# S5 and modulation transfers moved to the queues of the engines that produce the data, and one overlapping transfer per page of response matrices, in a kernel of two transformer blocks

## The chip, the cores and the metric

One NeuronCore of one Trainium2 chip. The metric is the device time of one execution in microseconds (us); several runs give a median.

## The reference, cut to what matters

The input is a sequence of 512 tokens of width 1024, in float32. The first block modulates its two normalisations by a projection of the condition c, and between them runs a hybrid of three mixers: S5 (a diagonal state space model of 32 groups, 16 channels and 64 states each), MLA (low-rank attention with 8 heads) and a spatial gating unit. Their outputs are gated and projected. The second block has dilated attention, mLSTM and feed-forward parts, and is not touched.

```python
mod = silu(c) @ w_ada + b_ada              # six rows of 1024
proj = h @ w_in + b_in
u_s5, cq, ckv, k_pe, u_sgu, v_sgu, gate_logits = split(proj)
h_t = a * h_(t-1) + bb @ u_t               # S5, complex, per group
y_s5 = real(c @ h_t) + d * u
z = gelu(y_s5);  out = z * sigmoid(z @ w_glu + b_glu)
merged = sum over the branches of gates[b] * (y[b] @ w_branch[b])
return merged @ w_out
```

## The kernel before, in words

**Products in three passes.** Each float32 operand is split in a high part `whi` (ACT, L300) and a rest `wlo` (mostly DVE, L306), and each product is three matmuls (L315 to L317). Weights come as 512 KB pages `raw` (SP, L334). The large projections are written `fm` (features on the partitions) and `tm` (tokens on the partitions).

**How the order comes about.** The program is written out in Python, and each engine works through its own list in that order. The large projections are the foreground. Beside them run background generators (`Bg`, L44): at each piece of foreground matmul work the next step of each is written, up to its next `yield`; a rate of 1.0 makes two plain yields for 12 fm matmuls, and `yield 3` asks for a longer distance. S5, the modulation rows and the attention are three such generators. So what a generator writes stands, on each engine, between the casts and evictions of the foreground and of the other generators. Where an instruction has to wait, all that stands behind it on the same engine waits too. A pool of 36 pages of 4 KB per partition, 8 PSUM banks and 8 small tiles (`t2`) is used in turn: a new page waits for the last reader of the old one.

**Modulation.** `ada_rows` (L1118 to L1159) makes three rows of 1024 (parts j = 4, 3, 2). A part has eight steps k: a 128 x 1024 page `adaw` of w_ada is loaded (512 KB, SP, L1130), ACT multiplies it by a column of the condition (L1145), POOL adds it to `adaacc` (L1146), and the load of the next page is written behind that add. Two matmuls with ones (L1151) then sum over the partitions, DVE adds 1 or 0 (L1157), and SP stores the row (L1158). `ada_join` (L1161) combines two rows with the norm's gains and stores them (L1174). The first two parts run during the S5 stretch, the third in the attention. `ada_gen` (L1074 ff) makes other rows of the same matrix at about 656 to 715 us; its loads are issued by POOL (L1088).

**S5.** `s5_params` (L1196 ff) computes powers of the eigenvalues and the response of a step, `s5k`, which SP stores into the DRAM tile `s5kd` (L1366). The foreground's u5 projection is stored as `s5ud` by ACT. `s5_main` (L1425) reads it back in two halves h, 8 loads of 64 KB each (`s5u`, SP, L1523). For each half `g_pe` multiplies it into the states (`s5g`, L1440), DVE turns and scans, and `y_pe` forms the output `psy`: 16 matmuls with the response matrices `s5m` (L1490), and 32 with the states (L1497); the trace lists each of these matmuls, and those of s5g, twice. The response matrix of a page is a block triangle: `responses` (L1475) has POOL clear the page (L1478) and SP load eight pieces of growing height from `s5kd` (L1481), 16 loads per half. `y_el` copies `psy` on ACT (`s5ys`, L1508) and SP stores it in eight pieces (`s5yd`, L1510); `y_in` (L1517) reads the result back as `s5yf`.

**Gates and attention.** The foreground of this stretch are the 24 gate rows: fm matmuls, a tanh on ACT (`gt`, L2030) and a store that ACT issues (`gates`, L2031). `mla_gen` (L1706) loads its weights (`wvr` by POOL, L1715; `wmr` by SP), splits the value weights (`wvs`, ACT L1749 and DVE L1751), forms the values (`mv`), and then, per head, queries `mq` and keys `mk`, the rotation on DVE and POOL (`rsh`, `mqf`, L1659, L1660), the scores `ms`, and the softmax `mp` on ACT (L1829).

**Completion of transfers.** The transfers that SP and ACT issue share eight completion counters, taken in the order of the program: an issue waits for the one eight before it, whichever of the two engines issued that. By their place in that round the eighth and the ninth s5u load wait for the two gates stores that the program has just ahead of them, on ACT.

Of the kernel before, what the change touches and what calls it, by code (L numbers as in the profile page):

```python
# [16 lines left out]
P = 128  # L17
# [938 lines left out]
class Block1(Core):  # L956
# [161 lines left out]
    def ada_rows(self, parts, fused):  # L1118


        nc = self.nc
        wv = self.ins["w_ada"][0].rearrange("(k p) n -> p k n", p=P)
        loads = []

        def load(n):
            if n < len(parts) * KD:
                i, k = divmod(n, KD)
                j = parts[i][0]
                w = self.page(name="adaw")
                nc.sync.dma_start(w[:, :D], wv[:, k, j * D : (j + 1) * D])  # L1130
                loads.append(w)

        load(0)
        for i, (j, plus, row) in enumerate(parts):
            acc = self.page(name="adaacc")
            nc.gpsimd.memset(acc[:, :D], 0.0)
            nc.gpsimd.dma_start(acc[0:1, :D], self.ins["b_ada"][0:1, j * D : (j + 1) * D])
            for k in range(KD):
                yield
                w = loads.pop(0)  # L1140
                c = self.ccol[:, k : k + 1]
                if fused:
                    nc.vector.scalar_tensor_tensor(acc[:, :D], w[:, :D], c, acc[:, :D], op0=ALU.mult, op1=ALU.add)
                else:
                    nc.scalar.activation(w[:, :D], w[:, :D], AF.Copy, scale=c)  # L1145
                    nc.gpsimd.tensor_tensor(acc[:, :D], acc[:, :D], w[:, :D], op=ALU.add)  # L1146
                load(i * KD + k + 1)
                yield 4 if k == KD - 1 else 0
            pss = [self.ps("adac") for _ in range(2)]
            for half in range(2):  # L1150
                nc.tensor.matmul(  # L1151
                    pss[half][0:1, :], self.ones[:, 0:1], acc[:, half * 512 : half * 512 + 512], start=True, stop=True
                )
            yield
            for half in range(2):
                r = self.t2(name="adar")[0:1, :]
                nc.vector.tensor_scalar(r, pss[half][0:1, :], plus, None, op0=ALU.add)  # L1157
                nc.sync.dma_start(row[:, half * 512 : half * 512 + 512], r)  # L1158
            yield  # L1159

    def ada_join(self, sc, sh):  # L1161

        nc = self.nc
        z = self.t2(name="adaz")[:8].rearrange("b (i p) -> b i p", i=4)
        for i, src in enumerate((sc, sh, self.ins["ln1_g"], self.ins["ln1_b"])):
            nc.sync.dma_start(z[:, i, :], src[0].rearrange("(b p) -> b p", p=P))
        yield
        yield 4
        yield
        nc.vector.tensor_tensor(z[:, 3, :], z[:, 0, :], z[:, 3, :], op=ALU.mult)  # L1170
        nc.vector.tensor_tensor(z[:, 1, :], z[:, 1, :], z[:, 3, :], op=ALU.add)
        nc.vector.tensor_tensor(z[:, 0, :], z[:, 0, :], z[:, 2, :], op=ALU.mult)
        for i, dst in enumerate((sc, sh)):
            nc.sync.dma_start(dst[0].rearrange("(b p) -> b p", p=P), z[:, i, :])  # L1174
        yield

    def vec_cols(self):
# [18 lines left out]
    def s5_params(self):  # L1196
# [137 lines left out]
            nc.vector.tensor_tensor(pw[:, 1, :, m + 1 : 2 * m + 1], x0[:, 1], x1[:, 0], op=ALU.add)  # L1334
        yield
        self.s5W = [[], []]
        self.s5kd = self.dr.tile([P, 512], F32, name="s5kd")
        for h in range(2):
            w, parts = self.s5_powers(h, 0, t0, t1, False)
            for f in parts:  # L1340
                yield
                f()
                yield 3
            for c in range(2):

                pss = [self.ps("s5wt") for _ in range(2)]
                for i in range(8):
                    nc.tensor.transpose(
                        pss[i // 4][:, i % 4 * P : i % 4 * P + P], w[c][:, i].rearrange("p k c -> p (k c)"), self.ident
                    )  # L1350
                if c == 0:
                    pk = [self.ps("s5k") for _ in range(2)]
                    for i in range(8):
                        for g in range(2):
                            hs = slice(64 * g, 64 * g + 64)
                            for e in range(2):
                                nc.tensor.matmul(
                                    pk[g][:, i : P : 8], w[e][hs, i].rearrange("p k c -> p (k c)"),
                                    cc[hs, e, 8 * h + i, :], start=e == 0, stop=e == 1,
                                )  # L1360
                yield
                if c == 0:
                    kk = self.t2(256, name="s5k")
                    for g in range(2):
                        nc.scalar.copy(kk[:, P * g : P * g + P], pk[g][:, :P])
                    nc.sync.dma_start(self.s5kd[:, 256 * h : 256 * h + 256], kk)  # L1366
                pg = self.page([P, 8, P], name="s5W")
                for j in range(2):
                    nc.scalar.copy(pg[:, 4 * j : 4 * j + 4].rearrange("p i s -> p (i s)"), pss[j])
                self.s5W[c].append(pg)  # L1370
                yield
            del w
# [52 lines left out]
    def s5_main(self, uf, ud, yd, yf):  # L1425
# [1 line left out]


        nc = self.nc
        U, V, M, G, A, B, Y = [], None, {}, {}, {}, {}, {}  # L1430
        tabs, cc, W = self.s5_tab, self.s5cc, self.s5W
        del self.s5_tab, self.s5cc, self.s5W

# [37 lines left out]
            nc.vector.tensor_tensor(A[h][:, 1], A[h][:, 1], B[h][:, 0], op=ALU.add)  # L1471
            del B[h]

        def responses(h):

            for g in range(2):
                M[g] = self.page([P, P, 8], name="s5m")
                nc.gpsimd.memset(M[g], 0.0)  # L1478
                ks = slice(256 * h + P * g, 256 * h + P * g + P)
                for t in range(8):  # L1480
                    nc.sync.dma_start(  # L1481
                        M[g][16 * (7 - t) :, 16 * t : 16 * t + 16, :],
                        self.s5kd[: 16 * t + 16, ks].rearrange("p (c i) -> p c i", i=8),
                    )

        def y_pe(h):
            Y[h] = [self.ps("psy") for _ in range(2)]
            for i in range(8):
                for g in range(2):
                    nc.tensor.matmul(  # L1490
                        Y[h][g][:, 64 * i : 64 * i + 64], M[g][:, :, i], U[h][:, 2 * i + g, :], start=i == 0, stop=False
                    )
            for i in range(8):
                for c in range(2):
# [8 lines left out]
        def y_el(h):  # L1503
# [3 lines left out]
            for g, y in enumerate(Y.pop(h)):  # L1507
                nc.scalar.copy(yv[:, g], y.rearrange("p (i n) -> p i n", i=8))  # L1508
            for t in range(8):
                nc.sync.dma_start(  # L1510
                    yd[256 * h : 256 * h + 256, 64 * t : 64 * t + 64].rearrange("(g c) n -> c g n", c=16),
                    ys[16 * t : 16 * t + 16],
                )
# [6 lines left out]
        for h in range(2):  # L1520
            U.append(self.page([P, 16, 64], name="s5u"))
            for s in range(8):
                nc.sync.dma_start(  # L1523
                    U[h][16 * (7 - s) : 16 * (8 - s)],
                    ud[256 * h : 256 * h + 256, 64 * s : 64 * s + 64].rearrange("(g c) n -> c g n", c=16),
                )
        yield 3
        for h in range(2):
            g_pe(h)
# [8 lines left out]
        for h in range(2):  # L1538
# [5 lines left out]
            yield 3  # L1544
            yield
            vs[1]()
            responses(h)
            yield 3
            y_pe(h)
            yield  # L1550
            y_el(h)
            del V, vs, A[h]
            if h == 0:
# [152 lines left out]
    def mla_gen(self, prep, res):  # L1706
# [30 lines left out]
                wsp[p] = (hi, lo)  # L1737

        load_w(0)
        yield  # L1740

        kps = [self.page([P, 2, 512], name="kT") for _ in range(2)]
# [1420 lines left out]
```

## Time and profile before

| | us |
|---|---|
| median of 3 runs | 2568.47 |
| lowest and highest | 2568.18, 2572.43 |
| the profiled execution | 2567.72 |
| its span in the trace | 2566.0 |

Share of the span in which each engine was busy: PE 95%, weight loads of PE 78%, DVE 50%, ACT 37%, POOL 12%. The mean granted clock of TensorE is 0.97 of full speed. The profiled execution lies 0.75 us under the median; 1.7 us of it lie outside the span. An engine's share is an average over 2566 us; the change touches the stretch from about 60 to 420 us, so the timelines and windows of that stretch are the views to read, and times in them are counted from the span's start.

### The profile page before, as it was taken

The numbers are of one execution on the slowest core, as the hardware profiler recorded it, in microseconds if no ns is written. First come the engines' busy times: TensorE is split into PE (matmuls) and PEld (weight loads), VectorE is DVE, ScalarE is ACT, GpSimd is POOL, SyncE is SP. The second block draws the span as 40 slices with busy tenths as digits, with TensorE's granted clock in tenths as the row PEclk, the third lists the DMA queues.
The fourth block names the chain that finished last, engine by engine and source line by source line (L and its number), as shares of the span: only waits on it lengthen the run. The fifth ranks groups of instructions, "written<-read, shape, count | busy, mean of one in ns | idle before, by whom it ended". The sixth has DMA issues, their size and how long they took to land.

```text
span 2566.0 us, 31035 instructions
## 1 busy us (share of the span) xinstructions
PE 2433.2 (95%) x11944; PEld 2008.4 (78%) x11944; DVE 1284.2 (50%) x2169; ACT 958.9 (37%) x1648; POOL 299.9 (12%) x340
## 2 busy tenths in 40 slices
PE   6967689998899999999999999999999999999998
PEld 5866567677788888888888888888888767888887
DVE  6775434468544438555545555333345556432333
ACT  4342245633222234555445453222233444322231
POOL 1032242001200000112111110000000232000000
PEclk9987789999899999999999999999999999999999
DMA  9243443363333325232323343233232214323321
GB/s 299 73 146 112 126 147 106 99 203 117 117 110 105 91 87 168 60 100 81 100 78 93 91 116 99 78 117 90 81 120 66 58 50 131 107 80 110 96 73 53
DMA packets 336149, 271.62 MB, mean 106 GB/s; under 512 B 33234, under 2 KB 288870, under 8 KB 336000
## 3 DMA queue, kind: packets, MB, share of 16 engines
q1 hardware_dynamic: 328832, 252.78, 32.8%
q0 software_dynamic: 3168, 9.51, 1.1%
q10 hardware_dynamic: 4000, 7.34, 0.8%
q8 instruction: 94, 1.54, 0.3%
q14 instruction: 55, 0.45, 0.1%
HBM read 252.50 MB, written 12.87 MB: 103 GB/s over the span
## 4 chain that ended last, share of the span: by engine, by line
PE 83%; DVE 8%; ACT 3%; issue 2%; DMA 2%; POOL 2%; SPq 1%; ACTq 0%; DVEq 0%; POOLq 0%
PE fm L315 16%; PE fm L316 16%; PE fm L317 16%; PE tm L315 9%; PE tm L317 9%; PE tm L316 8%; DVE wlo L306 1%; PE mo L1867 1%; PE ms L1805 1%; PE psy L1490 1%; PE ao L2534 1%; PE as L2408 1%; PE tr L750 1%; PE psy L1497 1%; DMA adaw<-in_w_ada_dram 1%
## 5 line engine op out<-in xcount | busy, mean ns | idle before, releaser
L315 PE MATMUL fm<-xT,whi 128*128 128x512 f32 (+1 forms) x1744 | 664.9, 381 | 0.3 <-ACT xT L300 0.2
L317 PE MATMUL fm<-xT,wlo 128*128 128x512 f32 (+1 forms) x1744 | 658.8, 378 | 4.4 <-DVE wlo L306 4.4
L316 PE MATMUL fm<-xT,whi 128*128 128x512 f32 (+1 forms) x1744 | 657.7, 377 | 0.8 <-DVE xT L306 0.7
L306 DVE TENSOR_TENSOR wlo<-raw,whi 128x1024 fp32r<-128x1024 f32 (+4 forms) x445 | 485.2, 1125 | 81.0 <-ACT whi L300 48.8
L300 ACT CAST whi<-raw 128x1024 fp32r<-128x1024 f32 (+3 forms) x447 | 393.5, 920 | 140.4 <-PE tm L316 50.4
L317 PEld LDWEIGHTS fm<-xT,wlo 128*128 128x128 f32 x1744 | 331.9, 190 | 67.2 <-DVE wlo L306 4.6
L315 PEld LDWEIGHTS fm<-xT,whi 128*128 128x128 f32 x1744 | 332.4, 191 | 62.6 <-issue 1.5
L316 PEld LDWEIGHTS fm<-xT,whi 128*128 128x128 f32 x1744 | 332.2, 191 | 60.9 <-DVE xT L306 1.5
L902 DVE TENSOR_TENSOR sl<-sl,fm 128x512 f32<-128x512 f32 x66 | 45.4, 688 | 426.6 <-PE fm L317 414.0
L315 PE MATMUL tm<-whi,hid 128*128 128x512 f32 x528 | 208.5, 395 | 0.0
L317 PE MATMUL tm<-whi,hid 128*128 128x512 f32 x528 | 207.8, 394 | 0.0
L316 PE MATMUL tm<-wlo,hid 128*128 128x512 f32 x528 | 207.6, 393 | 0.0
L901 ACT ACTIVATE sl<-fm 128x512 f32<-128x512 f32 x66 | 39.5, 599 | 383.7 <-PE fm L317 383.7
L317 PEld LDWEIGHTS tm<-whi,hid 128*128 128x128 f32 x528 | 99.2, 188 | 23.3
L316 PEld LDWEIGHTS tm<-wlo,hid 128*128 128x128 f32 x528 | 99.2, 188 | 22.9
L315 PEld LDWEIGHTS tm<-whi,hid 128*128 128x128 f32 x528 | 99.1, 188 | 22.9
L315 PE MATMUL tm<-whi,xT 128*128 128x384 f32 (+1 forms) x320 | 113.8, 356 | 0.0
L317 PE MATMUL tm<-whi,xT 128*128 128x384 f32 (+1 forms) x320 | 111.5, 348 | 0.0
L316 PE MATMUL tm<-wlo,xT 128*128 128x384 f32 (+1 forms) x320 | 111.3, 348 | 0.0
L315 PE MATMUL fm<-hT,whi 128*128 128x512 f32 x256 | 110.1, 430 | 0.7 <-ACT whi L300 0.7
L317 PE MATMUL fm<-hT,wlo 128*128 128x512 f32 x256 | 103.9, 406 | 7.2 <-DVE wlo L306 7.2
L300 ACT CAST hid<-sl 128x512 fp32r<-128x512 f32 x66 | 41.0, 621 | 186.8 <-DVE sl L902 186.8
(588 smaller groups left out, 3448.3 us busy)
## 6 DMA issues: line engine op xcount, KB each, us to landing
raw<-in_ffn_w_in_dram SPq DMA_DIRECT2D x264, 256.0 KB, 3.4
raw<-in_ffn_w_out_dram SPq DMA_DIRECT2D x69, 512.0 KB, 3.6
raw<-in_attn_w_in_dram SPq DMA_DIRECT2D x96, 256.0 KB, 3.4
adaw<-in_w_ada_dram SPq DMA_DIRECT2D x40, 512.0 KB, 5.9
raw<-in_w_in_dram SPq DMA_DIRECT2D x36, 512.0 KB, 4.8
raw<-in_attn_w_in_dram SPq DMA_DIRECT2D x96, 128.0 KB, 2.7
raw<-in_mlstm_w_in_dram SPq DMA_DIRECT2D x24, 512.0 KB, 3.8
gates<-gt ACTq DMA_DIRECT2D x24, 256.0 KB, 3.7
```

The costliest lines, as they stand in the source:

```text
L300: nc.scalar.copy(hi, src)
L306: f = lambda: eng.tensor_tensor(lo, src, hi.bitcast(F32), op=ALU.subtract)
L315: nc.tensor.matmul(out, a[0], b[0], start=start, stop=False)
L316: nc.tensor.matmul(out, a[0], b[1], start=False, stop=False)
L317: nc.tensor.matmul(out, a[1], b[0], start=False, stop=stop)
L750: self.nc.tensor.transpose(ps[:, (k - k0) * P : (k - k0 + 1) * P], src[:, k * P : (k + 1) * P], self.ident)
L901: nc.scalar.activation(s, ps[0], AF.Silu)
L902: nc.vector.tensor_tensor(s, s, ps[1], op=ALU.mult)
L1490: nc.tensor.matmul(Y[h][g][:, 64 * i : 64 * i + 64], M[g][:, :, i], U[h][:, 2 * i + g, :], start=i == 0, stop=False)
L1497: nc.tensor.matmul(Y[h][g][:, 64 * i + 1 : 64 * i + 64], V[c][hs, i].rearrange("p k c -> p (k c)"), A[h][hs, c, 64 * i : 64 * i + 63], sta ...
L1805: nc.tensor.matmul(ss_[i][:, :n], qts[h][:96, t * P : t * P + P], kts(h)[:, :n], start=True, stop=True)
L1867: nc.tensor.matmul(ops_[h][:, b * P :], vst[b][:, ds], pts_.pop(j), start=b == 0, stop=b == NT - 1)
```

## The change

Five things are done; lines are those of the changed kernel.

1. The 24 loads `adaw` are issued by POOL (L1130), each behind the add of the page before. The row is drained by ACT (L1158, L1160) instead of DVE and stored by ACT (L1161); the two stores of `ada_join` are issued by POOL (L1177).
2. The two stores of `s5k` are issued by ACT (L1373).
3. `s5kd` gets 112 rows of zeros ahead of its 128 (POOL clears and stores them once). `load_m` loads one page `s5r` with one transfer of 512 KB whose rows overlap in DRAM: partition p of block t begins at row p + 16 t. SP issues two of them for the first half right behind the s5u loads, and two for the second half behind the first `y_pe` (L1487). `responses` copies a page to `s5m` with the order of the columns changed (ACT, L1492) instead of POOL's clearing and 16 loads per half; the stationary operand of the matmul is contiguous.
4. The 16 stores `s5yd` are issued by ACT (L1520), behind its copies.
5. `mla_gen` has two more yields, one of them long, behind its first weight load.

```diff
                 w = self.page(name="adaw")
-                nc.sync.dma_start(w[:, :D], wv[:, k, j * D : (j + 1) * D])
+                nc.gpsimd.dma_start(w[:, :D], wv[:, k, j * D : (j + 1) * D])
...
                 r = self.t2(name="adar")[0:1, :]
-                nc.vector.tensor_scalar(r, pss[half][0:1, :], plus, None, op0=ALU.add)
-                nc.sync.dma_start(row[:, half * 512 : half * 512 + 512], r)
+                if plus:
+                    nc.scalar.activation(r, pss[half][0:1, :], AF.Identity, bias=self.ones[0:1, 0:1])
+                else:
+                    nc.scalar.copy(r, pss[half][0:1, :])
+                nc.scalar.dma_start(row[:, half * 512 : half * 512 + 512], r)
...
-            nc.sync.dma_start(dst[0].rearrange("(b p) -> b p", p=P), z[:, i, :])
+            nc.gpsimd.dma_start(dst[0].rearrange("(b p) -> b p", p=P), z[:, i, :])
...
-        self.s5kd = self.dr.tile([P, 512], F32, name="s5kd")
+
+        self.s5kd = self.dr.tile([112 + P, 512], F32, name="s5kd")
+        z = self.t2(name="s5z")[:112]
+        nc.gpsimd.memset(z, 0.0)
+        nc.gpsimd.dma_start(self.s5kd[:112], z)
...
-                    nc.sync.dma_start(self.s5kd[:, 256 * h : 256 * h + 256], kk)
+                    nc.scalar.dma_start(self.s5kd[112:, 256 * h : 256 * h + 256], kk)
...
-        def responses(h):
+        def load_m(h):
 
             for g in range(2):
-                M[g] = self.page([P, P, 8], name="s5m")
-                nc.gpsimd.memset(M[g], 0.0)
-                ks = slice(256 * h + P * g, 256 * h + P * g + P)
-                for t in range(8):
-                    nc.sync.dma_start(
-                        M[g][16 * (7 - t) :, 16 * t : 16 * t + 16, :],
-                        self.s5kd[: 16 * t + 16, ks].rearrange("p (c i) -> p c i", i=8),
-                    )
+                R[g] = self.page([P, 8, P], name="s5r")
+                src = self.s5kd[:P, 256 * h + P * g : 256 * h + P * g + P]
+                (r, _), (c, _) = src.ap
+                nc.sync.dma_start(R[g], bass.AP(src.tensor, src.offset, [[r, P], [16 * r, 8], [c, P]]))
+
+        def responses():
+            for g in range(2):
+                M[g] = self.page([P, 8, P], name="s5m")
+                nc.scalar.copy(
+                    M[g].rearrange("p i (t c) -> p t c i", t=8), R[g].rearrange("p t (c i) -> p t c i", i=8)
+                )
...
-                        Y[h][g][:, 64 * i : 64 * i + 64], M[g][:, :, i], U[h][:, 2 * i + g, :], start=i == 0, stop=False
+                        Y[h][g][:, 64 * i : 64 * i + 64], M[g][:, i, :], U[h][:, 2 * i + g, :], start=i == 0, stop=False
...
-                nc.sync.dma_start(
+                nc.scalar.dma_start(
                     yd[256 * h : 256 * h + 256, 64 * t : 64 * t + 64].rearrange("(g c) n -> c g n", c=16),
...
+        load_m(0)
         yield 3
...
-            responses(h)
+            responses()
...
+            if h == 0:
+                load_m(1)
             y_el(h)
...
         load_w(0)
+        yield
+        yield 3
         yield
```

Three places in the engines' lists. First POOL, where `ada_rows` begins; before:

```order
L1136 MEMSET adaacc_1201 128x1024
L1137 DMA adaacc_1201<-in_b_ada_dram 1x16x64
L1146 TENSOR_TENSOR adaacc_1201<-adaacc_1201,adaw_1199 128x1024
L1146 TENSOR_TENSOR adaacc_1201<-adaacc_1201,adaw_1218 128x1024
L1146 TENSOR_TENSOR adaacc_1201<-adaacc_1201,adaw_1260 128x1024
L1146 TENSOR_TENSOR adaacc_1201<-adaacc_1201,adaw_1302 128x1024
```

and with the change:

```order
L1130 DMA adaw_1202<-in_w_ada_dram 128x1024
L1136 MEMSET adaacc_1204 128x1024
L1137 DMA adaacc_1204<-in_b_ada_dram 1x16x64
L1146 TENSOR_TENSOR adaacc_1204<-adaacc_1204,adaw_1202 128x1024
L1130 DMA adaw_1221<-in_w_ada_dram 128x1024
L1146 TENSOR_TENSOR adaacc_1204<-adaacc_1204,adaw_1221 128x1024
L1130 DMA adaw_1263<-in_w_ada_dram 128x1024
L1146 TENSOR_TENSOR adaacc_1204<-adaacc_1204,adaw_1263 128x1024
L1130 DMA adaw_1305<-in_w_ada_dram 128x1024
```

Each add is now followed by the load of the page that the next add needs.

Second ACT, from the last gates store ahead of the second part of `ada_rows` up to the copies for the first half's `psy`. Before:

```order
L2031 DMA gates<-gt_1728 128x512
L1145 ACTIVATE adaw_1502<-adaw_1502,ccol 128x1024
L300 CAST cqT_1737<-cT_1708 128x512
L1145 ACTIVATE adaw_1735<-adaw_1735,ccol 128x1024
L300 CAST cqT_1766<-cT_1745 128x512
L300 CAST whi_1769<-raw_1511 128x1024
L1145 ACTIVATE adaw_1764<-adaw_1764,ccol 128x1024
L300 CAST cqT_1799<-cT_1778 128x512
L1145 ACTIVATE adaw_1797<-adaw_1797,ccol 128x1024
```

and with the change:

```order
L2046 DMA gates<-gt_1735 128x512
L1145 ACTIVATE adaw_1505<-adaw_1505,ccol 128x1024
L300 CAST cqT_1744<-cT_1715 128x512
L1145 ACTIVATE adaw_1742<-adaw_1742,ccol 128x1024
L300 CAST cqT_1773<-cT_1752 128x512
L300 CAST whi_1776<-raw_1514 128x1024
L1145 ACTIVATE adaw_1771<-adaw_1771,ccol 128x1024
L300 CAST cqT_1806<-cT_1785 128x512
L1492 COPY s5m_1814<-s5r_1534 128x128x8
L1492 COPY s5m_1816<-s5r_1536 128x128x8
L1145 ACTIVATE adaw_1804<-adaw_1804,ccol 128x1024
```

The two copies from `s5r` to `s5m` stand behind three scales of `adaw`.

Third SP, from the s5u loads to the response matrices of the first half. Before:

```order
L1523 DMA s5u_1513<-s5ud 16x16x64 x8
L1523 DMA s5u_1522<-s5ud 16x16x64 x8
L334 DMA raw_1609<-in_w_in_dram 128x4x256
L1158 DMA adarow_265<-adar_1687 1x512
L1158 DMA adarow_265<-adar_1690 1x512
L334 DMA raw_1698<-in_w_in_dram 128x4x256
L1130 DMA adaw_1735<-in_w_ada_dram 128x1024
L1130 DMA adaw_1764<-in_w_ada_dram 128x1024
L334 DMA raw_1772<-in_w_in_dram 128x4x256
L1130 DMA adaw_1797<-in_w_ada_dram 128x1024
L1481 DMA s5m_1807<-s5kd 16x128
L1481 DMA s5m_1807<-s5kd 32x128
```

and with the change:

```order
L1533 DMA s5u_1516<-s5ud 16x16x64 x8
L1533 DMA s5u_1525<-s5ud 16x16x64 x8
L1487 DMA s5r_1534<-s5kd 128x8x128
L1487 DMA s5r_1536<-s5kd 128x8x128
L334 DMA raw_1616<-in_w_in_dram 128x4x256
L334 DMA raw_1705<-in_w_in_dram 128x4x256
L334 DMA raw_1779<-in_w_in_dram 128x4x256
```

The stores of the modulation row and its loads have gone from between s5u and the response matrices, and the two loads `s5r` stand directly behind s5u.

## Rows read from the trace of the kernel before

**Rows 1.** Timeline of PE, 178 to 327 us: start, duration, line, operation; wait.

```profile
197.24 3.68 PE L1440 MATMUL s5g<-s5u,s5W 128*64 128x64 f32 x64 [13.57 <-DMA s5u<-s5ud]
...
232.93 0.71 PE L1490 MATMUL psy<-s5u,s5m 128*128 128x64 f32 x2 [6.47 <-DMA s5m<-s5kd]
236.82 7.38 PE L1490 MATMUL psy<-s5u,s5m 128*128 128x64 f32 x30 [3.18 <-DMA s5m<-s5kd]
...
280.33 0.71 PE L1490 MATMUL psy<-s5u,s5m 128*128 128x64 f32 x2 [11.99 <-DMA s5m<-s5kd]
286.09 7.37 PE L1490 MATMUL psy<-s5u,s5m 128*128 128x64 f32 x30 [5.05 <-DMA s5m<-s5kd]
...
324.25 0.80 PE L315 MATMUL mv<-wvs,cqT 128*128 128x512 f32 x1 [6.21 <-ACT wvs L1749]
326.42 0.79 PE L316 MATMUL mv<-wvs,cqT 128*128 128x512 f32 x1 [1.38 <-DVE wvs L1751]
```

**Rows 2.** Windows of four stretches: width, busy time by engine, granted clock (PEclk).

```profile
142.30:156.80 14.50, 10.90 (x72) 10.43 (x71) 13.10 (x14) 7.28 (x12) 5.37 (x2) 0.88 0.48 146
...
276.00:303.00 27.00, 17.62 (x102) 16.77 (x103) 6.03 (x6) 2.48 (x4) 1.84 (x2) 0.50 0.18 43
320.00:331.00 11.00, 5.37 (x12) 3.90 (x13) 5.09 (x6) 3.36 (x4) 1.95 (x1) 0.53 0.42 124
331.00:400.00 69.00, 64.94 (x275) 49.92 (x274) 25.62 (x59) 37.97 (x68) 34.47 (x19) 0.98 0.49 150
```

**Rows 3.** Groups by line of the tile adaw, 100 to 420 us; ns.

```profile
L1130 SPq DMA_DIRECT2D adaw<-in_w_ada_dram x24: 327/349/566, 133.0 to 386.3; - x24
L1145 ACT ACTIVATE adaw<-adaw,ccol x24: 1132/1148/1159, 140.7 to 390.8; 128x1024 f32<-128x1024 f32 x24
L1146 POOL TENSOR_TENSOR adaacc<-adaacc,adaw x24: 2358/2470/3274, 141.9 to 392.1; 128x1024 f32<-128x1024 f32 x24
...
DMA to landing us min/median/max: 4.8/5.1/5.3
```

**Rows 4.** The same for ada_gen's line L1088 on POOL, 600 to 760 us.

```profile
L1088 POOL DMA_DIRECT2D adaw<-in_w_ada_dram x8: 527/527/553, 655.9 to 715.3; - x8
...
DMA to landing us min/median/max: 3.9/4.2/5.1
```

**Rows 5.** Timeline of ACT: scales (L1145), a gates store, an idle time.

```profile
140.72 1.14 ACT L1145 ACTIVATE adaw<-adaw,ccol 128x1024 f32<-128x1024 f32 x1
...
142.32 1.15 ACT L1145 ACTIVATE adaw<-adaw,ccol 128x1024 f32<-128x1024 f32 x1
...
156.77 1.14 ACT L1145 ACTIVATE adaw<-adaw,ccol 128x1024 f32<-128x1024 f32 x1
...
187.80 2.17 ACT L1145 ACTIVATE adaw<-adaw,ccol 128x1024 f32<-128x1024 f32 x2
...
192.94 0.34 ACTq L2031 DMA_DIRECT2D gates<-gt  x1
...
214.78 1.16 ACT L1145 ACTIVATE adaw<-adaw,ccol 128x1024 f32<-128x1024 f32 x1 [0.40 <-ACT gt L2030]
...
254.55 1.15 ACT L1145 ACTIVATE adaw<-adaw,ccol 128x1024 f32<-128x1024 f32 x1 [0.48 <-ACT gt L2030]
...
269.12 1.15 ACT L1145 ACTIVATE adaw<-adaw,ccol 128x1024 f32<-128x1024 f32 x1 [1.50 <-DMA adaw<-in_w_ada_dram]
...
359.65 1.15 ACT L1145 ACTIVATE adaw<-adaw,ccol 128x1024 f32<-128x1024 f32 x1 [0.40 <-ACT gt L2030]
...
376.70 1.18 ACT L1793 COPY kT<-mk 64x512 f32<-64x512 f32 x2 [7.21 <-PE mk L317]
...
390.81 1.15 ACT L1145 ACTIVATE adaw<-adaw,ccol 128x1024 f32<-128x1024 f32 x1 [1.18 <-DMA adaw<-in_w_ada_dram]
```

**Rows 6.** SP's queue: timeline of the s5u loads, and SP's waits.

```profile
170.64 30.01 SPq L1523 DMA_DIRECT2D s5u<-s5ud  x16
...
SPq L1523 <- DMA gates<-gt: 20.4, 2, 19.6
```

More of the change, by code (lines that the diff above doesn't have):

```diff
@@ L1429, in s5_main @@
         nc = self.nc
-        U, V, M, G, A, B, Y = [], None, {}, {}, {}, {}, {}
+        U, R, M, G, A, B, Y = [], {}, {}, {}, {}, {}, {}
         tabs, cc, W = self.s5_tab, self.s5cc, self.s5W
```

## Prediction, made before the changed kernel was run

> **What bounds the kernel now.** TensorE is busy for 95% of the span (the table above), so time can only be won where it stands still or runs at its lower clock, and it is lost wherever the change makes it stand still anew. I read the timeline of PE first, for the stalls in the stretch that the change touches (140 to 400 us). There the reader is to see five waits [rows 1]: 13.57 us ahead of the first s5g for the DMA s5u; 6.47 and 3.18 us in the first y step, 11.99 and 5.05 us in the second, all four for the DMA s5m (26.7 in all); and 6.21 and 1.38 us ahead of mv, on ACT's and DVE's split of wvs. After each the clock is low: the windows from 276 to 303 and from 320 to 331 us have a granted clock of 0.50 and 0.53 of full speed, that is the 1.2 GHz level for nearly all of it, where 331 to 400 us has 0.98 [rows 2].
>
> The second view is the groups by line of the tile adaw, since the change puts 24 of its transfers elsewhere: the scale on ACT takes 1.15 us (L1145), the add on POOL 2.36 to 3.27, median 2.47 (L1146), and the load issued by SP lands in about 5.1 [rows 3]. POOL issues such loads already, in ada_gen: eight at 0.53 us each, landing in 3.9 to 5.1 us, median 4.2 [rows 4]. The third is ACT's timeline, which shows when the 24 scales run [rows 5], the fourth SP's own queue, where the 16 s5u loads take 30.01 us, 19.6 of it in one wait for the store of gates that ACT issues at 192.94 [rows 5, 6].
>
> **The change, part by part.** *The modulation loads.* Before, a load went into SP's queue and started as soon as a page was free, while POOL was still adding. Now load k+1 stands on POOL's queue behind add k, add k waits for scale k, and scale k for load k. Nothing of the three overlaps any more: one k costs 1.15 + 2.47 + 4.2 = 7.8 us, and up to 8.3 if the landing counts from the issue's end [rows 3, 4]. I take 8.0. ACT works in order and stands at each scale until its load has landed, with everything queued behind: the casts whi, the gates, the copies for S5, the softmax. So each stretch of eight k asks for seven gaps of 8.0 us, 56 us. It has to be compared with the time that the program leaves for it now, in three places [rows 5]:
>
> - First eight, 140.72 to 188.9 (the second of the pair at 187.80): the second scale moves from 142.32 to 148.7, the third from 156.77 to between 156.8 (the work between absorbs it) and 163.2 (all of it shifts); I take 159: in the 14.5 us between the two ACT is busy for 7.28, which alone would give 156.0, and DVE, whose results ACT's sine tables wait for, for 13.10 [rows 2]. Five more gaps of 8.0 put the last at 199, 10 us late. Behind it on ACT stands the gates store of 192.94, and behind that store the eighth s5u load, for which s5g already waits 13.57 us. Nothing covers it: **+10 us** (bounds +8 and +14).
> - Second eight, 214.78 to 269.12, which holds both y steps. The new s5m copies stand on ACT behind the third and the eighth scale. The first y: counted in times of before, with the 10 us above left out, 214.78 + 2 x 8.0 = 230.8, scale and add 3.6 (the second s5m page is one that the third add lets go), two copies at the price of the scale, same shape, 2.3: 236.7. Before, the wait ended at 236.82, with 0.7 us of psy already done [rows 1]. So +0.6 to +2. The second y: the fifth scale at 254.55 moves by the 1.5 us just lost and by eight s5yd issues of 0.34 (the price of the gates store) to 258.8; 3 x 8.0, scale, cast and two copies (4.5) give 287.2 against 286.09. So the 16 loads and two memsets that were waited for go, and ACT, held by the loads of adaw, is late in their place: **+2 us together**. The bound below is a gain of 22, the 26.7 less four copies; above, with a gap of 9.5 (both maxima), it is +6.
> - Third eight, 359.65 to 390.81: 31.2 us where 56 are asked, so the last scale comes 24.8 us later. In this stretch TensorE is busy 64.94 of 69 us [rows 2] and takes kT, mqf and mp from ACT and the rotated rows from POOL, in whose queue they stand behind the adds. ACT's idle time, 7.21 us at 376.70 [rows 5] and some 3 in smaller pieces, is what absorbs: **+15 us** (bounds 0, if the attention steps run ahead of the background far enough, and +25).
>
> *Response matrices.* The 32 SP issues and four POOL memsets go, four SP loads of 512 KB and four ACT copies come; the loads are issued behind s5u and one half ahead of y, so they lie beside other work. The costs are in the lines above. The matmuls stay, only their stationary operand is contiguous now: nothing, with a bound of the same 7 us a step if it mattered to the weight load.
>
> *s5yd on ACT, s5kd on ACT, row drains.* The 16 issues of s5yd cost ACT 2 x 2.7 us; the first eight are counted, the second eight stand before gates and casts that have slack. SP no longer waits there, but its weight loads are early anyway. The row drain's ACT work is 4 small operations beside a stalled ACT: nothing, bound +2. The zeroed 112 rows come early, one memset and one store: nothing.
>
> *The yields in the attention.* 36 gate matmuls now stand ahead of mv: at 64.94 / 275 = 0.236 us each [rows 2] 8.5 us of work that fills the 6.21 + 1.38 us wait, and keeps the clock up for the 12 matmuls from 320 to 331, which took 5.37 us, 2.5 more than at 0.236: together up to 10, of which I take **-9 us** (bounds -10 and 0, if ACT comes to wvs later by as much).
>
> Sum: +10 + 2 + 15 - 9 = +18 on the profiled execution's 2567.7 us, 2586. The median of the runs lies 0.75 us above that execution, which changes nothing here.
>
> The Trainium skill, "DMA: Bandwidth & Descriptors", section on issuing engines that are not separate DMA queues, says that issuing on another engine only saves issue time. By that alone the moves would be worth next to nothing either way and the sum would be that of the first rival below; the trace shows that what stands ahead of the issue on its engine matters too, as SP's 19.6 us wait for gates shows [rows 6]. The same page's section on SWDGE and HWDGE speaks against the change: loads issued by GpSimd can be held up by VectorE, those of SP and ACT cannot. The eight such loads here land no later than SP's, 3.9 to 5.1 us [rows 3, 4], so the trace does not bear it out.
>
> **Rivals.**
> 1. *Faster: the loads keep pace.* If scale k+1 rarely finds its load missing, ACT reaches the s5m copies in time, the 26.7 us of psy waits shrink to the four copies (-22), mv gives its 9, and no stretch adds: 2567.7 - 31 = **2537**, or some 7 us a step less again if the clock stays up. It decides at the gap: 6.9 us in the first stretch (48.2 in seven), 7.8 in the second, 4.5 in the third. For it: before, ACT waited for loads only now and then, and the second stretch needs just 0.2 us. Against it: even the shortest landing gives 1.15 + 2.36 + 3.9 = 7.4.
> 2. *Mixed: the y steps gain, the other two stretches cost.* As the second stretch is nearly wide enough, -22 there with +10, +15 and -9: **2561**.
> 3. *About the same: the third stretch hides behind TensorE's own work.* +10 + 2 - 9: **2571**.
> 4. *Worse: nothing absorbs in the third stretch,* and gaps of 8.3 or more: +14 + 6 + 25 - 9: **2604**.
> That the change does not do what it says is possible in one place: s5u still waits for the gates store of ACT, so freeing SP does not free it. The forecast has that in it.
>
> **How the numbers follow.** About 0.2% (5 us) is what a measurement of this kernel can tell from no change. Forecast 0.45, at 2586; rival 1 0.18, rival 2 0.15, rival 3 0.12, rival 4 0.10. Slower: the forecast, rival 4 and a part of rival 3, 0.60. Same: the rest of rival 3 and an edge of rival 2, 0.12. Faster: 0.28. The range goes from 2548 (rival 2 with its y steps' clock regained, leaving out most of rival 1) to 2606 (rival 4). The forecast's own range, from its bounds on the slower side, is 2574 to 2604.
>
> **What would show it.** Right: scales on ACT about 8 us apart, each idle before it on the DMA adaw; the s5g wait grown to 20 us or more behind a gates store near 203; psy waiting for ACT's s5m copy instead of the DMA; no wait ahead of mv; new PE waits in the attention steps on ACT or POOL. Wrong: psy starting without a wait, or scales 5 us apart or less with ACT never idle on adaw; then the first rival holds.

## The result, and the profile after

| | us |
|---|---|
| median before (4 runs) | 2568.32 |
| median after (4 runs) | 2591.64, from 2587.18 to 2592.47 |
| ratio after to before | 1.0085, interval 1.0067 to 1.0102 |
| span and mean granted clock of the profiled execution, before | 2566.0, 0.97 |
| the same, after | 2590.0, 0.964 |

The change makes the kernel slower by some 23 us, 0.85%. TensorE's busy time is 2433.2 us before and 2434.9 after: the loss is standing still.

The timeline of PE of the changed kernel, the rows that answer to [rows 1], with the waits that are new in the attention:

```profile
173.41 0.50 PE L315 MATMUL fm<-hT,whi 128*128 128x512 f32 x1 [3.85 <-ACT whi L300]
...
185.43 0.79 PE L317 MATMUL fm<-hT,wlo 128*128 128x512 f32 x1 [11.28 <-DVE wlo L306]
...
214.51 3.68 PE L1447 MATMUL s5g<-s5u,s5W 128*64 128x64 f32 x64 [24.44 <-DMA s5u<-s5ud]
...
252.37 0.69 PE L1500 MATMUL psy<-s5u,s5m 128*128 128x64 f32 x2 [8.41 <-ACT s5m L1492]
254.53 5.81 PE L1500 MATMUL psy<-s5u,s5m 128*128 128x64 f32 x26 [1.48 <-ACT s5m L1492]
...
304.19 0.69 PE L1500 MATMUL psy<-s5u,s5m 128*128 128x64 f32 x2 [18.75 <-ACT s5m L1492]
305.95 6.66 PE L1500 MATMUL psy<-s5u,s5m 128*128 128x64 f32 x30 [1.07 <-ACT s5m L1492]
...
346.18 0.39 PE L315 MATMUL mv<-wvs,cqT 128*128 128x512 f32 x1
...
374.75 0.79 PE L1820 MATMUL ms<-kT,mqf 96*128 96x128 f32 x2 [5.54 <-POOL mqf L1673]
...
395.49 0.47 PE L315 MATMUL mq<-cqT,wmh 128*96 128x512 f32 x1 [2.92 <-ACT wmh L300]
...
398.75 0.74 PE L317 MATMUL mq<-cqT,wml 128*96 128x512 f32 x1 [2.55 <-POOL wml L306]
```

The s5g wait has grown from 13.57 to 24.44 us, with two waits of 3.85 and 11.28 in front of it (the trace of before has 0.74 and 7.24 us there). The four psy waits are still there: 8.41 + 1.48 + 18.75 + 1.07 = 29.7 us where they were 26.7, but what they wait for is now ACT's copy, no longer a transfer. There is no wait ahead of mv. And the attention has new ones on POOL's mqf and on ACT's wmh.

What ACT does in that time is in its timeline, to be read against [rows 5]: scales (L1145), the first gates store, the copies to s5m (L1492).

```profile
143.43 1.13 ACT L1145 ACTIVATE adaw<-adaw,ccol 128x1024 f32<-128x1024 f32 x1
...
151.85 1.15 ACT L1145 ACTIVATE adaw<-adaw,ccol 128x1024 f32<-128x1024 f32 x1 [6.72 <-DMA adaw<-in_w_ada_dram]
...
161.89 1.14 ACT L1145 ACTIVATE adaw<-adaw,ccol 128x1024 f32<-128x1024 f32 x1
...
202.66 1.15 ACT L1145 ACTIVATE adaw<-adaw,ccol 128x1024 f32<-128x1024 f32 x1 [6.61 <-DMA adaw<-in_w_ada_dram]
...
206.77 0.34 ACTq L2046 DMA_DIRECT2D gates<-gt  x1
...
233.12 1.15 ACT L1145 ACTIVATE adaw<-adaw,ccol 128x1024 f32<-128x1024 f32 x1 [0.43 <-ACT gt L2045]
...
240.99 1.15 ACT L1145 ACTIVATE adaw<-adaw,ccol 128x1024 f32<-128x1024 f32 x1 [6.25 <-DMA adaw<-in_w_ada_dram]
...
248.82 1.15 ACT L1145 ACTIVATE adaw<-adaw,ccol 128x1024 f32<-128x1024 f32 x1 [5.25 <-DMA adaw<-in_w_ada_dram]
...
250.34 1.97 ACT L1492 COPY s5m<-s5r 128x1024 f32<-128x1024 f32 x1
252.50 1.97 ACT L1492 COPY s5m<-s5r 128x1024 f32<-128x1024 f32 x1 [0.19 <-POOL adaacc L1146]
...
300.18 1.15 ACT L1145 ACTIVATE adaw<-adaw,ccol 128x1024 f32<-128x1024 f32 x1 [6.97 <-DMA adaw<-in_w_ada_dram]
...
302.17 3.73 ACT L1492 COPY s5m<-s5r 128x1024 f32<-128x1024 f32 x2
...
360.00 1.15 ACT L1145 ACTIVATE adaw<-adaw,ccol 128x1024 f32<-128x1024 f32 x1 [0.46 <-ACT gt L2045]
...
418.06 1.15 ACT L1145 ACTIVATE adaw<-adaw,ccol 128x1024 f32<-128x1024 f32 x1 [4.20 <-DMA adaw<-in_w_ada_dram]
```

Inside a stretch the scales follow each other after about 8 us (143.43, 151.85; 233.12, 240.99, 248.82), with ACT idle before most of them until the load of adaw lands; the scale at 161.89, which other work holds back to 10 us behind the one before it, is an exception. Before, the second came 1.6 us after the first. The copies to s5m stand, with one cast between, behind a scale that waited 5.25 us (248.82) or 6.97 us (300.18). Groups by line of the tile adaw, to be read against [rows 3]:

```profile
L1130 POOL DMA_DIRECT2D adaw<-in_w_ada_dram x24: 553/570/607, 126.7 to 413.7; - x24
...
  DMA adaw<-in_w_ada_dram: 95.5, 19
...
DMA to landing us min/median/max: 3.8/4.2/6.3
```

The second line is ACT's idle time until an adaw load landed: 95.5 us in 19 waits, so 19 of 24 scales found their page missing; in the trace of before it was 14.2 us in 6 waits. The transfers themselves are no slower than SP's were: 4.2 us median to landing, 5.1 then.

### The profile page after: what moved, and what is told of

Same layout as the page of the kernel before. It is cut to its first block, busy times and chain, and to the rows that moved or that the text cites. A ratio compares the mean times of both kernels' runs of the same rounds, so it can differ in the third digit from the quotient of the medians.

```text
span 2590.0 us, 30996 instructions
## 1 busy us (share of the span) xinstructions
PE 2434.9 (94%) x11944; PEld 2009.7 (78%) x11944; DVE 1274.2 (49%) x2163; ACT 970.7 (37%) x1658; POOL 307.4 (12%) x364
## 4 chain that ended last, share of the span: by engine, by line
PE 78%; DVE 6%; DMA 5%; issue 4%; ACT 4%; POOL 2%; SPq 0%; ACTq 0%; DVEq 0%; POOLq 0%
PE fm L315 15%; PE fm L316 15%; PE fm L317 15%; PE tm L315 8%; PE tm L317 8%; PE tm L316 8%; DMA adaw<-in_w_ada_dram 3%; POOL adaacc L1146 1%; DVE wlo L306 1%; PE mo L1882 1%; ACT adaw L1145 1%; PE tr L750 1%; PE ao L2549 1%; PE as L2423 1%; PE psy L1507 1%
```

## The experiments

Twelve kernels were run, each beside the kernel before on the same chip; the ratio is to that kernel's runs. "Theory A" is the forecast's: load, scale and add follow each other with no overlap, and ACT stands at each scale. Its rivals are that ACT's own new work costs the time (B), and that POOL's queue as such does (C). The kernel before measured 2567.19 us beside experiments 1 to 4, 2570.31 beside 6, 7, 8 and 11, and 2566.91 beside 5, 9, 10 and 12, so a difference between experiments of different groups is good to some 3 us at best.

**1. All adaw loads back on SP, the rest of the change kept.**

```diff
-                nc.gpsimd.dma_start(w[:, :D], wv[:, k, j * D : (j + 1) * D])
+                nc.sync.dma_start(w[:, :D], wv[:, k, j * D : (j + 1) * D])
```

> The changed kernel with one line put back: the 24 adaw loads are issued by SP again, everything else stays. Theory A (the loss is the chain load, scale, add, in which nothing overlaps once the load stands behind the add on POOL): the scales no longer stand 7.8 to 8.2 us apart, the s5g wait falls from 24.4 to about 13, the two psy waits on the s5m copies from 29.7 to under 10 us, the attention's new waits go, and the time falls below that of before, to 2537 to 2552 us. Theory B (the loss is ACT's new work: copies to s5m, 16 issues of s5yd, the row drains): the time stays above 2575 us, and ACT is busy, not waiting, ahead of psy.

Measured: 2539.61 us, ratio 0.9895 (0.9879 to 0.9912). One line turns a loss of 23 us into a gain of 28, so B falls as the cause of the loss. Its PE timeline:

```profile
197.65 3.69 PE L1447 MATMUL s5g<-s5u,s5W 128*64 128x64 f32 x64 [13.50 <-DMA s5u<-s5ud]
...
229.52 0.43 PE L1500 MATMUL psy<-s5u,s5m 128*128 128x64 f32 x2 [2.06 <-ACT s5m L1492]
236.44 6.66 PE L1500 MATMUL psy<-s5u,s5m 128*128 128x64 f32 x30 [6.48 <-ACT s5m L1492]
...
269.76 0.43 PE L1500 MATMUL psy<-s5u,s5m 128*128 128x64 f32 x2 [3.00 <-ACT s5m L1492]
274.51 6.66 PE L1500 MATMUL psy<-s5u,s5m 128*128 128x64 f32 x30 [4.32 <-ACT s5m L1492]
```

The s5g wait is back at 13.50 us. The psy waits are 15.9 us in all, half of what they were but more than the 10 expected; experiments 9 and 10 find a part of the rest.

**2. Loads on POOL, one page further ahead.**

```diff
         load(0)
+        load(1)
...
-                load(i * KD + k + 1)
+                load(i * KD + k + 2)
```

> The changed kernel with the adaw loads still issued by POOL, but one page further ahead: two loads are issued at the start, and behind add k stands load k+2. Theory A (nothing overlaps): a load now lies beside one scale and one add, a step costs some 4 us instead of 8, less than the 6.9, 7.8 and 4.5 us that the three stretches leave, so the time falls to 2537 to 2555 us, close to that of the run with the loads on SP. Theory C (it is the queue of POOL itself: software transfers that land late or hold up VectorE): the time stays above 2575 us though the order is changed.

Measured: 2542.49 us, ratio 0.9906 (0.9891 to 0.9921). Groups by line of the tile adaw in that run:

```profile
L1130 POOL DMA_DIRECT2D adaw<-in_w_ada_dram x24: 532/569/607, 128.6 to 365.1; - x24
...
  DMA adaw<-in_w_ada_dram: 14.9, 5
```

The loads are still POOL's, and ACT waits 14.9 us for them in 5 places instead of 95.5 in 19; in the kernel before, with SP's loads, it was 14.2 in 6. So C falls as the cause of the loss: this run and the first differ by 3 us, within the intervals. In the two traces it is 6.2 us from the first scale to the projection behind the attention, and 3.4 of them have another place: here two adaw loads (195.22 and 198.10) are in flight with the gates stores (the first at 196.54), which land in 4.0 us, and s5g, at 204.19, waits 16.86 us; experiment 8 takes that up. What costs is that the load stood behind the add of the page before with nothing in flight.

**3. The kernel before with adaw on POOL, nothing else.**

```diff
-                nc.sync.dma_start(w[:, :D], wv[:, k, j * D : (j + 1) * D])
+                nc.gpsimd.dma_start(w[:, :D], wv[:, k, j * D : (j + 1) * D])
```

> The kernel before with one line changed: the 24 adaw loads are issued by POOL, behind the add. Theory A: slower by the first and third stretch, 17 us each as the trace of the changed kernel has them, and by what ACT's lateness costs the y steps, little since the copies on ACT are absent here; 2595 to 2612 us. The mv wait of 6.2 and 1.4 us stays. Theory B (ACT's new work): within 5 us of 2568.

Measured: 2626.39 us, ratio 1.0233 (1.0217 to 1.0248): 59 us slower, well above what was expected. A reason is on POOL's timeline:

```profile
248.85 2.33 POOL L1146 TENSOR_TENSOR adaacc<-adaacc,adaw 128x1024 f32<-128x1024 f32 x1 [4.99 <-ACT adaw L1145]
251.14 0.57 POOL L1130 DMA_DIRECT2D adaw<-in_w_ada_dram  x1
251.70 1.86 POOL L1478 MEMSET s5m<- 128x1024 f32 x2
```

In the kernel before, POOL also clears the pages s5m, and the clearing stands behind the third and the eighth add. Those adds are late now, so SP's 16 loads into the page start late, and TensorE waits for them, 43.9 us in all against 26.7 [rows 1]:

```profile
258.69 0.71 PE L1490 MATMUL psy<-s5u,s5m 128*128 128x64 f32 x2 [14.89 <-DMA s5m<-s5kd]
...
318.17 0.71 PE L1490 MATMUL psy<-s5u,s5m 128*128 128x64 f32 x2 [22.17 <-DMA s5m<-s5kd]
```

I had left that link out. Measured in the two traces, from the first scale to s5g, from there to the last psy group, and from there to the first matmul of the projection behind the attention (tm<-mT), this kernel is slower by 13.5, 17.7 and 27.2 us: the middle figure is that link, and the third stretch costs 10 us more than was expected, for which I have no separate run. It means that in the change itself the response matrices took back a part of what the adaw loads cost.

**4. The kernel before with the response matrices alone.** The diff is the part of the change on s5kd, load_m, responses and y_pe; s5kd is still stored by SP.

> The kernel before with the response matrices alone changed: zeroed rows in s5kd, two overlapping loads per half on SP, two ACT copies in place of the 16 loads and the memsets; all other transfers stay where they were. Theory A: the 26.7 us of psy waits on s5m shrink to the copies, so 2543 to 2552 us, with some us more if the clock stays up through psy. Theory B: no gain, the waits move to ACT's copies and stay above 20 us; 2565 to 2575 us.

Measured: 2549.23 us, ratio 0.9931 (0.9917 to 0.9946), a gain of 18 us as theory A has it; the psy waits are 13.3 us, all on ACT's copies.

**5. The kernel before with the two yields alone.**

```diff
         load_w(0)
         yield
+        yield 3
+        yield
```

> The kernel before with the two yields alone. The prediction's term: the waits of 6.2 and 1.4 us ahead of mv and the low clock behind them go, 9 us, so 2561 us; with the 3.7 us wait for wml in the same attention step, which is absent too where the yields were added to the response matrices, 2553 to 2558 us. The step from 2549.2 to 2529.2 us between the two runs with response matrices would ask for 20 us, 2550.

Measured: 2550.26 us, ratio 0.9929 (0.9909 to 0.9949): 17 us, with an interval of 13 to 23, where the prediction's term was 9. In its trace the 6.21 and 1.38 us ahead of mv are gone, and so is a wait for wml later in the attention, which the prediction had not counted. The timeline of PE of the kernel before has it:

```profile
371.88 0.74 PE L317 MATMUL mq<-cqT,wml 128*96 128x512 f32 x1 [3.71 <-POOL wml L306]
```

**6. The kernel before with response matrices and yields.**

> The kernel before with the response matrices and the two yields of the attention, and nothing else of the change: adaw, s5kd, s5yd, the row drains and ada_join's stores stay where they were. If the moves of the small transfers are worth nothing, as the prediction had it, 2537 to 2543 us, like the run of the changed kernel with adaw on SP (2539.6). If they help, 2545 us or more; the yields then give less than the 9 us of the mv wait and its clock on top of 2549.2.

Measured: 2529.20 us, ratio 0.9849 (0.9833 to 0.9866). The two add up: 18 + 17 = 35, against 39 measured by the ratio, within the intervals. It is 10 us faster than experiment 1, which has the moves of the small transfers besides. Neither branch of what was expected here had that: the moves of the small transfers, in experiment 1, cost, where the prediction put them at nothing.

**7. Only the third part's loads on POOL,** the first two parts' on SP.

```diff
-                nc.gpsimd.dma_start(w[:, :D], wv[:, k, j * D : (j + 1) * D])
+                eng = nc.gpsimd if len(parts) == 1 else nc.sync
+                eng.dma_start(w[:, :D], wv[:, k, j * D : (j + 1) * D])
```

> The changed kernel with the adaw loads of the first two parts issued by SP and only those of the third part, in the attention, by POOL behind the add. Theory A with stretches that add up: 15 to 18 us more than the 2539.6 of the run with all loads on SP, 2554 to 2558 us. If the attention's waits came only from the lateness that the earlier stretches had built up, less than 2547 us.

Measured: 2558.04 us, ratio 0.9959 (0.9944 to 0.9974), 18 us above experiment 1 by the medians, 16 by the ratios. In the traces it is 21.3: from the last psy group to the projection behind the attention this kernel takes 286.8 us and experiment 1 265.5. The same waits in the attention as in the changed kernel appear, though S5 is undisturbed:

```profile
340.60 0.79 PE L1821 MATMUL ms<-kT,mqf 96*128 96x128 f32 x2 [5.18 <-POOL mqf L1674]
...
362.34 0.74 PE L315 MATMUL mq<-cqT,wmh 128*96 128x512 f32 x1 [4.37 <-ACT wmh L300]
...
365.60 0.74 PE L317 MATMUL mq<-cqT,wml 128*96 128x512 f32 x1 [2.09 <-POOL wml L306]
```

**8. The load that opens the second part is written at that part's beginning.**

```diff
+            if i:
+                load(i * KD)
             acc = self.page(name="adaacc")
...
-                load(i * KD + k + 1)
+                if k < KD - 1:
+                    load(i * KD + k + 1)
```

> The changed kernel, with the one load that opens the second part of the modulation written at that part's beginning instead of behind the last add of the part before. In the changed kernel that load was in flight together with the gates store on which s5u waits, and the store landed in 5.1 us. If the two compete for the DMA engines, the store lands in 2 to 3 us, s5g starts some 3 us earlier, and the time falls by about 3 us, to 2587 to 2590. If the store is slow for another reason, its landing stays at 5 us and the time at 2591. Either way the 8 us chain stays.

Measured: 2584.97 us, ratio 1.0061 (1.0046 to 1.0076), the upper end of which overlaps the lower end of the changed kernel's (1.0067). The trace decides more sharply. DMA issues of the changed kernel from 204 to 216 us (count, KB each, median us to landing), and of this one from 195 to 208:

```profile
adaw<-in_w_ada_dram POOLq DMA_DIRECT2D x1, 512.0 KB, 5.0
gates<-gt ACTq DMA_DIRECT2D x2, 256.0 KB, 5.1
```

```profile
gates<-gt ACTq DMA_DIRECT2D x2, 256.0 KB, 2.0
```

By the medians the time fell by 6.7 us, more than the 3 expected. With the load out of the way the gates stores land in 2.0 us instead of 5.1. From the first gates store to s5g it is 4.19 us (202.32 to 206.51) instead of 7.74 (206.77 to 214.51); before it was 4.30. That is 3.6 of the 8.0 us by which s5g comes earlier; the other 4.4 lie ahead of the gates store, where the two programs are the same, and are a difference between two executions (2.7 of them ahead of the first scale, 140.73 here and 143.43 there).

**9. Experiment 1 with the row's drain on DVE and SP again.**

```diff
-                if plus:
-                    nc.scalar.activation(r, pss[half][0:1, :], AF.Identity, bias=self.ones[0:1, 0:1])
-                else:
-                    nc.scalar.copy(r, pss[half][0:1, :])
-                nc.scalar.dma_start(row[:, half * 512 : half * 512 + 512], r)
+                nc.vector.tensor_scalar(r, pss[half][0:1, :], plus, None, op0=ALU.add)
+                nc.sync.dma_start(row[:, half * 512 : half * 512 + 512], r)
```

> The changed kernel with adaw on SP and with the modulation row's drain put back too: DVE adds, SP stores. In the run with adaw on SP, ACT stood 14.3 us at the drain, waiting for the matmuls adac that TensorE reaches only behind s5g, and the copy s5dec behind it came at 213.95 instead of 203.66 as in the run with response matrices and yields alone (2529.2). If that costs the y steps: s5dec near 204, the two second psy waits (6.5 and 4.3) shorter by 2 to 3 us each, and 2532 to 2536 us instead of 2539.6. If DVE had slack there: 2539 to 2541 us.

Measured: 2534.25 us, ratio 0.9870 (0.9850 to 0.9889); the interval overlaps that of experiment 1. ACT's timeline of experiment 1, and the same copy s5dec in this one:

```profile
195.91 0.61 ACT L1468 COPY s5dec<-s5cols 128x512 f32<-128x512 f32 x1
210.79 0.68 ACT L1158 ACTIVATE adar<-adac,ones 1x512 f32<-1x512 f32 x1 [14.26 <-PE adac L1151]
...
213.95 0.62 ACT L1468 COPY s5dec<-s5cols 128x512 f32<-128x512 f32 x1
```

```profile
204.91 0.61 ACT L1465 COPY s5dec<-s5cols 128x512 f32<-128x512 f32 x1
```

The drain on ACT waited 14.26 us for matmuls that TensorE reaches only behind s5g, and held s5dec up by 9 us. From s5g to the start of the last group of psy it is 83.5 us there and 81.0 here: 2.5 us. Of the two waits that were to shrink, the first did (6.48 to 4.31 us) and the second did not (4.32, 4.33). The rest of the 5 us between the medians is within their spread.

**10. Experiment 1 with the s5yd stores on SP again.**

```diff
-                nc.scalar.dma_start(
+                nc.sync.dma_start(
                     yd[256 * h : 256 * h + 256, 64 * t : 64 * t + 64].rearrange("(g c) n -> c g n", c=16),
```

> The changed kernel with adaw on SP and with the s5yd stores on SP as well, the drain still on ACT. With the stores on ACT, ACT spends 3.9 us on eight issues and waits 3.95 more for one of them to land before it goes on to gt, twice. If TensorE depends on what stands behind: 2533 to 2536 us instead of 2539.6, with no wait of gt on s5yd. If the gates have slack: 2538 to 2541 us.

Measured: 2532.29 us, ratio 0.9863 (0.9847 to 0.9878). ACT no longer issues the eight stores nor waits behind them, and from s5g to the last psy group it is 81.3 us instead of 83.5. In experiment 6 it is 79.8, so drain and stores, 2.5 and 2.2 us, cover the 3.6 us by which the traces of experiments 1 and 6 differ in the y steps. The rest of the 10 us between their medians is not located.

**11. Experiment 1 with the s5u loads ahead of the gates stores.** They are written during the sine tables, as soon as u5 is there.

```diff
+            for x in self.s5_start():
+                if len(uf) == 4 and not U:
+                    load_u()
+                yield x
-            yield from self.s5_start()
```

> The changed kernel with adaw on SP again and with the 16 s5u loads written earlier, during the sine tables of S5, ahead of the first gates stores. If s5g's wait of 13.5 us is only the round of completion counters that ties the eighth s5u load to the gates store on ACT, the wait goes and the clock stays up: 2522 to 2532 us. If the data itself or the page is late, s5g waits on and the time stays at 2536 to 2544 us.

Measured: 2526.57 us, ratio 0.9835 (0.9819 to 0.9852), 13 us under experiment 1. In its PE timeline s5g starts with no wait at all:

```profile
187.59 2.53 PE L1447 MATMUL s5g<-s5u,s5W 128*64 128x64 f32 x64
```

So the wait of 13.57 us [rows 1] was the round of completion counters and neither the data nor the pages.

**12. Experiment 6 with the early s5u loads.**

> The kernel before with the response matrices, the yields and the early s5u loads: all three gains of the runs so far without the moved loads, drains and stores. If they add up: 2529.2 less the 13 us that the early loads gave on the changed kernel with adaw on SP, 2514 to 2519 us. If the y steps become the bound instead, because s5m is not ready earlier, 2522 to 2528 us.

Measured: 2524.95 us, ratio 0.9836 (0.9819 to 0.9853), the lowest median here and level with experiment 11 by the ratio, but only 4 us under experiment 6 where 10 to 15 were asked if the gains add up, with intervals that overlap; it is the second branch of what was expected. In the trace s5g comes 12.8 us earlier (183.34 against 196.09), and at the last psy group 7.3 of them are left (268.65 against 275.92): a new wait of 1.90 us on DVE's s5A stands in the first y step, and the first wait on s5m has grown from 2.31 to 6.93. At the projection behind the attention 6.6 us are still there (534.15 against 540.78). What follows is written the same in all kernels, and from there to the end the fourteen traces take between 1984.8 us (experiment 6) and 1991.9 (the kernel before), 1991.3 here: the rest is lost in the spread between executions.

## Why the prediction was right, and where it was not

The forecast was 2586, slower, by ACT being held in the modulation chain; measured were 2591.64. The mechanism is shown: one line moves some 50 us (experiment 1), and the same queue with one more page in flight comes within 3 us of it by the medians (experiment 2). Of the terms, the chain and the y steps are right, and the errors of the others partly cancel.

To place them I count from the first scale, since the stretch ahead of it differs between executions of the same program: experiment 5, which is the kernel before up to there, has its first scale at 144.26 us, the kernel before at 140.72, the changed one at 143.43. The first line is that scale in experiment 5, the others are the first matmul of the projection behind the attention, before and after:

```profile
144.26 1.14 ACT L1145 ACTIVATE adaw<-adaw,ccol 128x1024 f32<-128x1024 f32 x1
```

```profile
574.04 0.40 PE L315 MATMUL tm<-whi,mT 128*128 128x512 f32 x1
```

```profile
600.71 0.39 PE L315 MATMUL tm<-whi,mT 128*128 128x512 f32 x1
```

- **The gap of 8.0 us** was right: from the first to the last scale of the first eight 59.2 us, less the 10.0 between second and third that other work sets, 49.2 in six gaps, 8.2 each.
- **First stretch, +10 us: the chain right, a landing missing.** s5g came 17.3 us later (214.51 against 197.24), of which 2.7 lie ahead of the first scale and are no part of the change. From the first scale to the first gates store the chain took 11.1 us more, and 9.4 in experiment 8, the same program up to there. But 3.4 us were missing from the sum: the load for the next part goes out at 206.25, just before the gates store at 206.77, and with both in flight the store lands 3.1 us later. Experiment 8 shows that price by taking the load away. So the stretch is 14.6, just above its bound of 14.
- **The y steps, +2 us: right.** From the first s5g to the last psy group it was 96.2 us before and 98.0 after. Some of that is luck: a copy was priced at the scale's 1.15 us and took 1.97, and eight s5yd issues at 2.7 us and took 3.9, while the contiguous operand, put at nothing, took the 30 matmuls of a step from 7.38 us [rows 1] to 6.66, both at a granted clock of 0.50.
- **Third stretch, +15 us: too small.** Experiment 7 measures 18 against experiment 1 by the medians and 21.3 in the traces, within the bounds.
- **Yields, -9 us: too small.** Alone they give 17 (experiment 5), some 15 in its trace. The failed step is the list of what they cover: it named the mv waits and their clock, and not the wml wait of 3.71 us. In the changed kernel a wait for wml is there again, 2.55 us, as in experiment 7 (2.09), where experiment 1 has 0.19.
- **Drains and s5yd, "nothing, bound +2": wrong where ACT is not held by something else.** In experiment 1 they cost 2.5 and 2.2 us of the y steps. Whether they cost anything in the changed kernel, where ACT waits for loads anyway, no run shows.
- **Sum:** 14.6 to s5g, 1.9 in the y steps and 7.5 for third stretch and yields together make 24.0 us at the projection (574.04 - 140.72 = 433.3 before, 600.71 - 143.43 = 457.3 after), where the forecast had 10, 2 and 15 - 9 = 6. That the last pair came so close is luck: in the traces both of its terms were some 6 us or more too small, and they have opposite signs.

On the rivals: the first, 2537, is what the kernel does once its loads do keep pace, 2539.61 and 2542.49; its decision point was put rightly, and the gaps of 8.2 us are on the wrong side of it. The second, gains in the y steps alone, is refuted by their 29.7 us of waits, the third, a third stretch that hides, by experiment 7; the fourth asked for 25 us there, of which 18 to 21 came. The Trainium skill, "DMA: Bandwidth & Descriptors", section on issuing engines that are not separate DMA queues, has another issuer save no more than issue time. For the transfer as such the runs agree: experiments 1 and 2 differ by 3 us, within their intervals. For a kernel it is not enough: the same 24 issues cost 59 us where they stood behind the add (experiment 3). The Trainium skill's section on SWDGE and HWDGE, on the same page, has VectorE lock GpSimd out, in one of VectorE's modes, of the memory where GpSimd prepares its transfers. No run here singles that mode out; over the 24 loads there is no sign of it, with 4.2 us median to landing from POOL and 5.1 from SP.

## What to carry to other kernels

A load belongs on an engine whose earlier instructions do not wait for it or for its neighbours: put behind the consumer of the page before, it has nothing in flight, and the cost is the sum of load and use for every page, on each engine that works in order behind it. To price such a move, compare that sum with the time between uses in the stretch, and add what else is queued on the engine that waits. If the issuer has to be that engine, write the load one page further ahead. And look at what a load waits for through the round of completion counters: writing the s5u loads ahead of another engine's stores was worth 13 us in experiment 11, and 4 in experiment 12.

## What was not expected of the hardware

Two transfers of 256 and 512 KB in flight together slowed the smaller one from 2.0 to 5.1 us to landing (experiment 8; 4.0 beside two loads in experiment 2), which went straight to TensorE because a transfer eight places later, on another engine, was waiting for it. And a copy of 128 x 1024 float32 on ACT that reads its columns in order and writes them in a new one took 1.97 us, where the scale of the same shape takes 1.15; no run tells whether the order alone makes the difference.
